# Two feed-forward layers on one Trainium2 core: the last pair of the opening block computed plainly, and half of the second weight matrix's rows loaded through POOL's queue

## The chip, the cores and the metric

The program runs on one core of a Trainium2 chip. The metric is the device time of one execution in microseconds; lower is better. Before the change three executions took 2122.06 us in the median (2121.51 to 2124.43). The engines are called PE (the matmul engine), DVE (vector), ACT (scalar), POOL and SP; SP issues most of the DMAs, POOL issues some.

## The reference, cut to what matters

Two layers over 256 tokens of width 2048: layer 0 mixes tokens with an mLSTM, layer 1 with an RG-LRU. Each layer ends in the same kind of feed-forward network, which takes more than half of the time and is where the change lies:

```python
def swiglu(x, w_in, w_out):
    g, u = jnp.split(x @ w_in, 2, axis=-1)
    return (jax.nn.silu(g) * u) @ w_out
...
        h = h + mix
        h = h + swiglu(rms_norm(h, norm_ffn[layer]), ffn_w_in[layer], ffn_w_out[layer])
    return rms_norm(h, norm_final)
```

`w_in` is 2048 x 11264 (gate and up part side by side), `w_out` is 5632 x 2048, all in float32.

## The kernel before, in words

**Split operands.** Every float32 operand is cut into a rounded part and a remainder, `hi` and `lo`. A product is three matmuls (`product`, L828 to L830): hi times hi, hi times lo, lo times hi. So each weight tile costs ACT a rounding copy (L264, `hi`) and DVE a subtraction (L265, `lo = raw - hi`) before PE can use it.

**Blocks and pairs.** `ffn` walks over 11 blocks `j` of 512 hidden columns. `inner` computes one block: it walks over 8 pairs `p` of 128-row chunks of `w_in`, and for each pair `pairs` loads four 128x512 pieces by two DMAs on SP's queue (L299). Two ways of multiplying a pair exist. A *plain* pair takes 8 products (24 matmuls) and needs the four pieces split (`whi`, `wlo`, 128x2048). Any other pair takes 7 products (21 matmuls) by a Strassen-like scheme, which needs three of the pieces split (`whix`, `wlox`) and four sums of pieces formed by DVE (`sum`, L308, L311, L312) and split in two halves (`whit`, `wlot`: the first half holds T1 and T3, the second T2 and T4). The set `BOTH` names the pairs that are plain in block 0; pair 0 is always plain. A plain pair of `BOTH` needs two more activation tiles, which `NormPairs.pair` makes in the mixer before (`more`, L489 to L495).

**The end of a block.** After the last Strassen-like pair (7), the sums P1, Q6 and P7 are final and ACT and DVE combine them (L863 to L866); after the block follow the rest, two Silu (L873, L876) and two products (L878). `turn_v` (L887) transposes the result for the second matmul.

**The second matmul in pieces.** `outs` cuts block j's part of `w_out` into eight pieces: quarter q of the output columns, token block b. One piece is 12 matmuls, and `between` puts one behind some product of each pair, so that the pieces of one block run inside the next. Pieces are summed in `h`: `o` is filled with `h` (L946), 12 matmuls add to it, and a copy on ACT writes it back (L957). Two weight tiles serve the pieces of a quarter. Tile 0 is split as above. Tile 1 is split in another way: ACT writes the rounded negative of the rows (L925, `wl`), an accumulating DMA from POOL's queue adds the rows from memory to it (L926), so that `wl` becomes the remainder without DVE; a second ACT copy writes `wh` (L927). `rawo` has one buffer for each tile, `wl` of tile 1 has two in turn.

**Order.** A scheduler puts the instructions of each engine in a fixed order by priorities; `after(...)` adds a rule that an instruction comes behind another on its engine. Each engine and each queue then runs strictly in that order, so a wait holds up all that stands behind it. SP's queue holds the loads of `w_in` and `w_out`; POOL's queue holds the accumulating DMAs and a few small operations.

**Parameters.** Small vectors are loaded as rows, transposed on PE and kept in three 128x128 tiles `cols` (L178 to L211).

Of the kernel before, what the change touches and what calls it, by code (L numbers as in the profile page):

```python
# [8 lines left out]
F32 = mybir.dt.float32  # L9
# [19 lines left out]

SEVENS = (1, 2, 3, 4, 5, 6, 7)  # L30

BOTH = (1, 2, 3, 4)

SHIFT = 48
PRODUCTS = (
# [9 lines left out]
def kernel(  # L45
# [129 lines left out]

    rows = pool_of("y").tile([P, 4, T], F32, tag="yh3", name="rows")
    rows = [rows[:, i, 0:P] for i in range(3)]
    cols = [const.tile([P, P], F32, name=f"cols{i}") for i in range(3)]  # L178
    part, at, used, par_rows = 0, 0, [0, 0, 0], []
    for name, src, n in par_src:  # L180
        if part == 0 and at or at + n > P:
            part, at = part + 1, 0
        par_rows.append((rows[part][at:at + n, :], src))
        par[name] = cols[part][:, at:at + n]
        at += n
        used[part] = at
    bif = const.tile([H, 2], F32, name="bif")

    gain0 = cols[0][:, 64:68]
    nc.scalar.dma_start(gain0, norm_mix[0].rearrange("(k p) -> p k", p=P)[:, 0:4])  # L190
    load_x()
    nc.scalar.dma_start(*par_rows.pop(0))
# [11 lines left out]
        return order  # L204

    def par_cols(i):
        n = used[i]
        pt = misc(f"par{i}")
        nc.tensor.transpose(pt[:, 0:n], rows[i][0:n, :], ident[0:n, 0:n])
        with tc.high_priority(offset=AHEAD):  # L210
            nc.vector.tensor_copy(cols[i][:, 0:n], pt[:, 0:n])  # L211


    pending = []
# [235 lines left out]
    class NormPairs(Norm):  # L450
# [10 lines left out]
        def pair(self, p):  # L461
            plain = p not in SEVENS
            k0, k1 = 2 * p, 2 * p + 1
            order = ((k0, 0), (k0, 1), (k1, 0), (k1, 1)) if plain else ((k1, 1), (k0, 0), (k0, 1), (k1, 0))
            n = 6 if plain else 7
            pt = misc(f"tr_{self.name}{p}").rearrange("p (s t) -> p s t", t=P)
            for i, (k, b) in enumerate(order):
                nc.tensor.transpose(pt[:, i, :], h[:, b, k * P:(k + 1) * P], ident)
            place, tag = ("c", "c") if "c" in pools else ("rawo", "raw0")
            c = pool_of(place).tile([P, 10 if place == "c" else 8, P], F32, tag=tag, name=f"c_{self.name}{p}")  # L470
            for k, sl in ((k0, slice(0, 2)), (k1, slice(2, 4))) if plain else ((k0, slice(1, 3)), (k1, slice(0, 4, 3))):
                nc.scalar.activation(c[:, sl, :], pt[:, sl, :], AF.Copy, scale=self.gain[:, k:k + 1])
            if plain:
                nc.vector.tensor_tensor(c[:, 4:6, :], c[:, 0:4:2, :], c[:, 1:4:2, :], op=ALU.subtract)
                src = c[:, 0:6, :]
            else:

                nc.vector.tensor_tensor(c[:, 4, :], c[:, 0, :], c[:, 2, :], op=ALU.subtract)
                nc.vector.tensor_tensor(c[:, 5, :], c[:, 3, :], c[:, 0, :], op=ALU.subtract)
                nc.vector.tensor_tensor(c[:, 6, :], c[:, 3, :], c[:, 4, :], op=ALU.subtract)  # L480
                nc.vector.tensor_tensor(c[:, 7, :], c[:, 1, :], c[:, 6, :], op=ALU.subtract)
                src = c[:, 1:8, :]

            rest = SHIFT if p == NK // 2 - 1 else 0
            xt = pool_of("x").tile([P, 2 * n * P + rest], F32R, tag=f"p{p}", name=f"p{p}_{self.name}")
            xt = xt[:, 0:2 * n * P].rearrange("p (s n t) -> p s n t", s=2, n=n)
            split(xt[:, 0], xt[:, 1], src)
            self.x.append(xt)
            if p in BOTH:  # L489

                nc.scalar.copy(c[:, 8, :], c[:, 0, :])
                nc.vector.tensor_tensor(c[:, 9, :], c[:, 1, :], c[:, 2, :], op=ALU.subtract)
                more = pool_of("more").tile([P, 2, 2, P], F32R, tag=f"m{p}", name=f"m{p}_{self.name}")
                split(more[:, 0], more[:, 1], c[:, 8:10, :])
                self.more[p] = more  # L495

        def parts(self, q):
# [309 lines left out]
    def ffn(layer, n, nxt):  # L807
# [24 lines left out]
        def inner(j, between):  # L832
# [9 lines left out]

            ds = fp.tile([P, 4, NB], F32, tag="ds", name=f"ds{j}")
            d0, d1, s0, s1 = (ds[:, i, :] for i in range(4))
            for p, ops in pairs(w, j, layer == 1):
                if is_plain(j, p):

# [4 lines left out]
                else:  # L852
                    seven = n.seven(p)
                    work = [
                        (c, seven[a], ops[b], p == SEVENS[-1])
                        for c, a, b in (LAST if p == SEVENS[-1] else PRODUCTS)
                    ]
                for i, job in enumerate(work):
                    add(*job)
                    between(j, p, i + 1 - len(work))  # L860
                if p == SEVENS[-1]:
                    with tc.high_priority(offset=AHEAD):
                        nc.scalar.copy(s0, ps["P1"])  # L863
                        nc.vector.tensor_tensor(d0, ps["Q6"], s0, op=ALU.subtract)
# [25 lines left out]
            with tc.high_priority(offset=AHEAD):  # L890
                split_store(hi[:, 2 * i:2 * i + 2, :], lo[:, 2 * i:2 * i + 2, :], pt)

        fresh = [True]

        def outs(j, hi, lo):

# [6 lines left out]
            def load(q, last):  # L903
# [9 lines left out]
                for i in range(2):  # L913
# [4 lines left out]
                        for what, dt, at in (("raw", F32, ""), ("whi", F32R, ""), ("wlo", F32R, spare))  # L918
                    )
                    src = wv[:, 2 * i:2 * i + 2, q * NB:(q + 1) * NB]  # L920
                    nc.sync.dma_start(raw, src)
                    with tc.high_priority(offset=AHEAD):
                        if i:

                            nc.scalar.activation(wl, raw, AF.Copy, scale=-1.0)  # L925
                            nc.gpsimd.dma_start(wl, src, accum_op=ALU.add)  # L926
                            nc.scalar.copy(wh, raw)  # L927
                        else:
# [3 lines left out]
            def piece(q, b, last=False):  # L932
# [20 lines left out]
                with tc.high_priority(offset=AHEAD):  # L953
                    if first:
                        nc.vector.tensor_tensor(hs, o, hs, op=ALU.add)
                    else:
                        nc.scalar.copy(hs, o)  # L957

            return [(piece, q, b) for q in range(4) for b in range(NT)]

# [266 lines left out]
```

## Time and profile before

| what | before |
|---|---|
| median of three executions | 2122.06 us |
| profiled execution, its own time | 2119.97 us |
| span of the profile | 2118.2 us |
| granted PE clock, mean | 0.998 |
| PE busy, share of the span | 2074.1 us, 98% |
| DVE busy | 1756.5 us, 83% |
| ACT busy | 1438.4 us, 68% |
| POOL busy | 135.4 us, 6% |
| DMA moved | 446.66 MB, 211 GB/s |

In the profile a row reads: line, engine, operation, output<-inputs, shape, count. "[8.66 <-DMA rawo]" behind a row of the timeline is the time that the engine sat idle before it, and what ended the wait. Matmuls overlap each other, and their ends are modelled: a matmul of 512 columns is shown as 0.39 us, but the starts of undisturbed ones stand 0.2267 us apart. The first feed-forward network runs from 398.5 us on, the second from 1402.2 us on.

### The profile page before, as it was taken

Reading aid. Unit: us, or ns where it says so; the run is one execution under the profiler, and the core shown is the slowest. Engines: PE = TensorE matmul, PEld = TensorE weight load, DVE = VectorE, ACT = ScalarE, POOL = GpSimd, SP = SyncE. Lnnn points to the kernel's source line nnn. Section 1 sums busy time; section 2 is a strip of 40 time slices with the busy share of each in tenths; the row PEclk is TensorE's granted clock in tenths of the full one; section 3 lists DMA queues with packets and bytes.
Section 4 is the critical chain, followed back from the end, with each engine's and each line's share of the span. In section 5 each row is a group of like instructions: output and inputs, shape, how many; then the busy total and the mean of one; then the engine's idle time right before and its main releaser. Section 6 shows DMA issues by size and latency. Waiting matters only on the chain.

```text
span 2118.2 us, 27777 instructions
## 1 busy us (share of the span) xinstructions
PE 2074.1 (98%) x10418; PEld 1737.8 (82%) x10418; DVE 1756.5 (83%) x1936; ACT 1438.4 (68%) x1749; POOL 135.4 (6%) x140
## 2 busy tenths in 40 slices
PE   9999999989999999999999999998999999999998
PEld 8988888867888888887879999886788887888886
DVE  6655556599999999999986788669999999999996
ACT  5444446557777777777764778655777777777775
POOL 0011110000000000000000000000000000000001
PEclk9999999999999999999999999999999999999999
DMA  7556666656877878888765666764788887878874
GB/s 224 170 163 178 179 185 218 192 165 194 243 239 235 231 229 239 237 236 230 230 189 160 193 189 188 228 203 154 209 245 231 235 232 222 242 231 248 238 222 156
DMA packets 233119, 446.66 MB, mean 211 GB/s; under 512 B 16328, under 2 KB 17048, under 8 KB 232856
## 3 DMA queue, kind: packets, MB, share of 16 engines
q1 hardware_dynamic: 211048, 402.92, 58.3%
q0 software_dynamic: 21216, 40.90, 12.3%
q8 instruction: 81, 1.33, 0.3%
q10 hardware_dynamic: 720, 1.07, 0.1%
q14 instruction: 54, 0.44, 0.1%
HBM read 442.74 MB, written 2.10 MB: 210 GB/s over the span
## 4 chain that ended last, share of the span: by engine, by line
PE 80%; ACT 7%; DVE 6%; DMA 4%; issue 3%; POOL 0%; ACTq 0%; POOLq 0%; SPq 0%; DVEq 0%
PE out L828 6%; PE out L829 6%; PE out L830 6%; PE P L829 5%; PE P L830 5%; PE P L828 5%; PE Q L828 5%; PE Q L829 5%; PE Q L830 4%; DMA rawo<-in_ffn_w_out_dram 4%; PE po L324 3%; PE po L326 3%; PE po L325 3%; DVE wlox L265 2%; DVE wlot L265 1%
## 5 line engine op out<-in xcount | busy, mean ns | idle before, releaser
L240 DVE TENSOR_TENSOR wlo<-raw,whi 128x1024 fp32r<-128x1024 f32 (+1 forms) x226 | 273.5, 1213 | 171.5 <-ACT whi L239 169.0
L264 ACT CAST whit<-sum 128x1024 fp32r<-128x1024 f32 x292 | 305.5, 1049 | 108.0 <-DVE sum L308 87.7
L265 DVE TENSOR_TENSOR wlot<-sum,whit 128x1024 fp32r<-128x1024 f32 x292 | 355.0, 1221 | 23.6 <-ACT whit L264 22.7
L239 ACT CAST whi<-raw 128x1024 fp32r<-128x1024 f32 (+1 forms) x226 | 234.4, 1042 | 196.0 <-PE po L326 43.2
L828 PE MATMUL out<-whio,hh 128*128 128x512 f32 x704 | 275.1, 391 | 0.1
L829 PE MATMUL out<-wloo,hh 128*128 128x512 f32 x704 | 274.4, 390 | 0.0
L830 PE MATMUL out<-whio,hh 128*128 128x512 f32 x704 | 274.3, 390 | 0.0
L265 DVE TENSOR_TENSOR wlox<-raw,whix 128x1536 fp32r<-128x1536 f32 x146 | 256.0, 1754 | 13.8 <-ACT whix L264 13.2
L264 ACT CAST whix<-raw 128x1536 fp32r<-128x1536 f32 x146 | 216.0, 1480 | 26.0 <-PE P L830 22.3
L308 DVE TENSOR_TENSOR sum<-raw 128x1024 f32<-128x1024 f32 x146 | 178.6, 1224 | 10.0 <-DMA raw<-in_ffn_w_in_dram 5.9
L925 ACT ACTIVATE wloo<-rawo 128x1024 fp32r<-128x1024 f32 x78 | 82.8, 1062 | 144.3 <-DMA rawo<-in_ffn_w_out_dram 144.3
L926 POOL DMA_DIRECT2D wloo<-in_ffn_w_out_dram x78 | 94.0, 1206 | 1229.3 <-ACT wloo L925 918.9
L828 PEld LDWEIGHTS out<-whio,hh 128*128 128x128 f32 x704 | 132.1, 188 | 29.7 <-ACT out L946 1.2
L829 PEld LDWEIGHTS out<-wloo,hh 128*128 128x128 f32 x704 | 132.2, 188 | 28.0 <-DVE wloo L265 0.7
L830 PEld LDWEIGHTS out<-whio,hh 128*128 128x128 f32 x704 | 132.2, 188 | 27.7
L828 PE MATMUL Q<-whit,p_f 128*128 128x512 f32 x292 | 117.1, 401 | 12.5 <-ACT whit L264 12.5
L828 PE MATMUL P<-whix,p_f 128*128 128x512 f32 x292 | 114.8, 399 | 9.0 <-ACT whix L264 9.0
L264 ACT CAST whio<-rawo 128x1024 fp32r<-128x1024 f32 (+1 forms) x88 | 101.0, 1147 | 33.1 <-PE out L830 23.9
L265 DVE TENSOR_TENSOR wloo<-rawo,whio 128x1024 fp32r<-128x1024 f32 (+1 forms) x88 | 117.9, 1339 | 5.6 <-ACT whio L264 5.5
L829 PE MATMUL P<-wlox,p_f 128*128 128x512 f32 x292 | 115.3, 395 | 4.1 <-DVE wlox L265 3.8
L829 PE MATMUL P<-wlot,p_f 128*128 128x512 f32 x292 | 114.0, 390 | 1.7 <-DVE wlot L265 1.7
L830 PE MATMUL P<-whix,p_f 128*128 128x512 f32 x292 | 114.6, 393 | 0.0
(296 smaller groups left out, 5131.4 us busy)
## 6 DMA issues: line engine op xcount, KB each, us to landing
raw<-in_ffn_w_in_dram SPq DMA_DIRECT2D x352, 512.0 KB, 6.5
rawo<-in_ffn_w_out_dram SPq DMA_DIRECT2D x176, 512.0 KB, 5.7
raw<-in_m_w_in_dram SPq DMA_DIRECT2D x94, 512.0 KB, 3.8
wloo<-in_ffn_w_out_dram POOLq DMA_DIRECT2D x78, 512.0 KB, 6.3
raw<-in_r_w_in_dram SPq DMA_DIRECT2D x64, 512.0 KB, 4.3
raw<-in_m_w_out_dram SPq DMA_DIRECT2D x32, 512.0 KB, 3.7
raw<-in_r_w_out_dram SPq DMA_DIRECT2D x32, 512.0 KB, 4.5
gr<-in_r_gate_w_dram SPq DMA_DIRECT2D x8, 512.0 KB, 3.8
```

Of the source, the lines that this page charges most:

```text
L239: nc.scalar.copy(hi[:, i:i + step, 0:ncols], r)
L240: nc.vector.tensor_tensor(lo[:, i:i + step, 0:ncols], r, hi[:, i:i + step, 0:ncols].bitcast(F32), op=ALU.subtract)
L264: nc.scalar.copy(hi, src)
L265: nc.vector.tensor_tensor(lo, src, hi.bitcast(F32), op=ALU.subtract)
L308: nc.vector.tensor_tensor(t[:, 0:2, :], raw[:, 1:3, :], raw[:, 3:4, :].broadcast_to([P, 2, NB]), op=ALU.add)
L324: nc.tensor.matmul(o, lhsT=ah[:, bs], rhs=hi, start=(k == 0), stop=False)
L325: nc.tensor.matmul(o, lhsT=ah[:, bs], rhs=lo, start=False, stop=False)
L828: nc.tensor.matmul(o, lhsT=a[0], rhs=b[0], start=start, stop=False, **kw)
L829: nc.tensor.matmul(o, lhsT=a[0], rhs=b[1], start=False, stop=False, **kw)
L830: nc.tensor.matmul(o, lhsT=a[1], rhs=b[0], start=False, stop=stop, **kw)
L925: nc.scalar.activation(wl, raw, AF.Copy, scale=-1.0)
L926: nc.gpsimd.dma_start(wl, src, accum_op=ALU.add)
```

## The change

Six edits that hang together:

1. `BOTH` gets pair 7. In block 0 of each layer pair 7 is plain: 24 matmuls where 21 stood, no sums, one split of 128x2048. The last Strassen-like pair of that block is then 6 (`last`), and P1, Q6 and P7 are combined one pair earlier. The stop flags and the order of products follow.
2. The extra activation tiles are made in place in `c` (columns 0 and 1), so one ACT copy per pair of `BOTH` goes; pair 7 gets such a tile (`m7`).
3. The parameters lie in two `cols` tiles where three stood; with the smaller `c` this makes room for `m7`. As many transposes and copies as before.
4. The rows for tile 1 of the pieces are loaded by POOL's queue, not SP's.
5. The rounded negative of tile 1 (L925 before, L928 after) is put behind the copy back to `h` (L957, now L960) of the last piece but one that was written.
6. Line numbers move by one to three.

```diff
-BOTH = (1, 2, 3, 4)
+BOTH = (1, 2, 3, 4, 7)
...
-    cols = [const.tile([P, P], F32, name=f"cols{i}") for i in range(3)]
...
+    cols = [const.tile([P, P], F32, name=f"cols{i}") for i in range(2)]
...
-            c = pool_of(place).tile([P, 10 if place == "c" else 8, P], F32, tag=tag, name=f"c_{self.name}{p}")
+            c = pool_of(place).tile([P, 8, P], F32, tag=tag, name=f"c_{self.name}{p}")
...
-                nc.scalar.copy(c[:, 8, :], c[:, 0, :])
-                nc.vector.tensor_tensor(c[:, 9, :], c[:, 1, :], c[:, 2, :], op=ALU.subtract)
+                nc.vector.tensor_tensor(c[:, 1, :], c[:, 1, :], c[:, 2, :], op=ALU.subtract)
...
-                split(more[:, 0], more[:, 1], c[:, 8:10, :])
+                split(more[:, 0], more[:, 1], c[:, 0:2, :])
...
+            last = max(p for p in SEVENS if not is_plain(j, p))
...
-                        (c, seven[a], ops[b], p == SEVENS[-1])
-                        for c, a, b in (LAST if p == SEVENS[-1] else PRODUCTS)
+                        (c, seven[a], ops[b], p == (last if c in ("P7", "P1", "Q6") else NP - 1))
+                        for c, a, b in (LAST if p == NP - 1 else PRODUCTS)
...
-                if p == SEVENS[-1]:
+                if p == last:
...
-        fresh = [True]
+        fresh, copies = [True], []
...
-                    nc.sync.dma_start(raw, src)
+                    (nc.gpsimd if i else nc.sync).dma_start(raw, src)
...
-                            nc.scalar.activation(wl, raw, AF.Copy, scale=-1.0)
+                            with after(*copies[-2:-1]):
+                                nc.scalar.activation(wl, raw, AF.Copy, scale=-1.0)
                             nc.gpsimd.dma_start(wl, src, accum_op=ALU.add)
                             nc.scalar.copy(wh, raw)
...
-                        nc.scalar.copy(hs, o)
+                        copies.append(nc.scalar.copy(hs, o))
```

In the orders below a name such as `rawo011` reads: block 0, quarter 1, tile 1; `whix0_5` is block 0, pair 5; `whit4_7` block 4, pair 7; the number at the end is a buffer's.

POOL, at the start of the first feed-forward network, before:

```order
L440 TENSOR_TENSOR rstd_f0_3780<-ms_f0_3777,mhalf_93 128x2
L926 DMA wloo001_4215<-in_ffn_w_out_dram 128x2x512
L926 DMA wloo011_4333<-in_ffn_w_out_dram 128x2x512
L926 DMA wloo021_4461<-in_ffn_w_out_dram 128x2x512
L926 DMA wloo031_4598<-in_ffn_w_out_dram 128x2x512
```

and after:

```order
L923 DMA rawo001_4205<-in_ffn_w_out_dram 128x2x512
L442 TENSOR_TENSOR rstd_f0_3779<-ms_f0_3776,mhalf_93 128x2
L929 DMA wloo001_4207<-in_ffn_w_out_dram 128x2x512
L923 DMA rawo011_4323<-in_ffn_w_out_dram 128x2x512
L929 DMA wloo011_4325<-in_ffn_w_out_dram 128x2x512
L923 DMA rawo021_4451<-in_ffn_w_out_dram 128x2x512
```

The rows of the next quarter now stand behind the accumulating DMA of this one; SP's queue has lost these loads.

ACT, in block 0 of the first feed-forward network, from the second rounded negative on, before:

```order
L925 ACTIVATE wloo011_4333<-rawo011_4331 128x1024
L264 CAST p6_f0_3724<-c_f06_3717 128x896
L264 CAST whix0_5_3882<-raw0_5_3875 128x1536
L472 ACTIVATE c_f07_3763<-tr_f07_3758,cols1_97 128x256
L472 ACTIVATE c_f07_3763<-tr_f07_3758,cols1_97 128x2x128
L264 CAST p7_f0_3770<-c_f07_3763 128x896
L264 CAST whit0_5_3886<-sum0_5_3878 128x1024 x2
L264 CAST whio000_4208<-rawo000_4207 128x1024
L264 CAST whix0_6_3923<-raw0_6_3916 128x1536
L264 CAST whit0_6_3927<-sum0_6_3919 128x1024 x2
L264 CAST whix0_7_3961<-raw0_7_3954 128x1536
L264 CAST whit0_7_3965<-sum0_7_3957 128x1024
```

and after:

```order
L928 ACTIVATE wloo011_4325<-rawo011_4323 128x1024
L266 CAST whix0_5_3881<-raw0_5_3874 128x1536
L266 CAST p6_f0_3719<-c_f06_3712 128x896
L474 ACTIVATE c_f07_3758<-tr_f07_3753,cols0_96 128x256
L474 ACTIVATE c_f07_3758<-tr_f07_3753,cols0_96 128x2x128
L266 CAST whit0_5_3885<-sum0_5_3877 128x1024 x2
L266 CAST p7_f0_3765<-c_f07_3758 128x896
L266 CAST whix0_6_3922<-raw0_6_3915 128x1536
L266 CAST m7_f0_3769<-c_f07_3758 128x256
L266 CAST whit0_6_3926<-sum0_6_3918 128x1024 x2
L266 CAST whi0_7_3959<-raw0_7_3956 128x2048
```

The second negative still stands ahead of pair 5; the copy `whio000` has left the place ahead of pair 6, and pair 7 is one split.

ACT, in a later block (block 4, end of pair 6 and pair 7), before:

```order
L264 CAST whit4_6_5813<-sum4_6_5805 128x1024
L925 ACTIVATE wloo321_5970<-rawo321_5968 128x1024
L264 CAST whit4_7_5879<-sum4_7_5871 128x1024
L957 COPY h_73<-out310_5847 128x512
L264 CAST whit4_7_5879<-sum4_7_5871 128x1024
L946 COPY out311_5897<-h_73 128x512
L863 COPY ds4_5430<-P1_4_5525 128x512
```

and after:

```order
L266 CAST whit4_6_5805<-sum4_6_5797 128x1024
L266 CAST whix4_7_5867<-raw4_7_5860 128x1536
L266 CAST whit4_7_5871<-sum4_7_5863 128x1024
L960 COPY h_73<-out310_5839 128x512
L928 ACTIVATE wloo321_5962<-rawo321_5960 128x1024
L266 CAST whit4_7_5871<-sum4_7_5863 128x1024
L949 COPY out311_5889<-h_73 128x512
```

The negative `wloo321` has moved behind the copy of piece 310; it now stands between the two halves of pair 7.

ACT again, at the first Silu pair of the next block, before:

```order
L264 CAST whit5_1_6022<-sum5_1_6014 128x1024
L925 ACTIVATE wloo331_6107<-rawo331_6105 128x1024
L876 ACTIVATE ds4_5430<-ds4_5430,rstd_f0_3780 128x512
L957 COPY h_73<-out320_5975 128x512
L946 COPY out321_6041<-h_73 128x512
L264 CAST whit5_1_6022<-sum5_1_6014 128x1024
```

and after:

```order
L266 CAST whit5_1_6014<-sum5_1_6006 128x1024
L878 ACTIVATE ds4_5422<-ds4_5422,rstd_f0_3779 128x512
L266 CAST whit5_1_6014<-sum5_1_6006 128x1024
L960 COPY h_73<-out320_5967 128x512
L928 ACTIVATE wloo331_6099<-rawo331_6097 128x1024
```

The negative `wloo331` has left the place ahead of the second Silu and stands behind the copy of piece 320.

DVE, in block 4, pair 7, before:

```order
L265 TENSOR_TENSOR wlox4_7_5876<-raw4_7_5868,whix4_7_5875 128x1536
L265 TENSOR_TENSOR wlot4_6_5814<-sum4_6_5805,whit4_6_5813 128x1024
L308 TENSOR_TENSOR sum4_7_5871<-raw4_7_5868 128x1024
L311 TENSOR_TENSOR sum4_7_5871<-sum4_7_5871,raw4_7_5868 128x512
L312 TENSOR_TENSOR sum4_7_5871<-sum4_7_5871,raw4_7_5868 128x512
L265 TENSOR_TENSOR wlot4_7_5880<-sum4_7_5871,whit4_7_5879 128x1024 x2
```

and after:

```order
L267 TENSOR_TENSOR wlot4_6_5806<-sum4_6_5797,whit4_6_5805 128x1024
L310 TENSOR_TENSOR sum4_7_5863<-raw4_7_5860 128x1024
L267 TENSOR_TENSOR wlox4_7_5868<-raw4_7_5860,whix4_7_5867 128x1536
L313 TENSOR_TENSOR sum4_7_5863<-sum4_7_5863,raw4_7_5860 128x512
L267 TENSOR_TENSOR wlot4_7_5872<-sum4_7_5863,whit4_7_5871 128x1024
L314 TENSOR_TENSOR sum4_7_5863<-sum4_7_5863,raw4_7_5860 128x512
L267 TENSOR_TENSOR wlot4_7_5872<-sum4_7_5863,whit4_7_5871 128x1024
```

The third sum now stands behind the first half's subtraction, and nothing stands between it and the second half's.

PE, in block 4, at the start of pair 7, before:

```order
L830 MATMUL P1_4_5525<-whix4_7_5875,p7_f0_3770 128x512
L828 MATMUL P7_4_5553<-whit4_7_5879,p7_f0_3770 128x512
L828 MATMUL Q6_4_5557<-whit4_7_5879,p7_f0_3770 128x512
L829 MATMUL P7_4_5553<-wlot4_7_5880,p7_f0_3770 128x512
L830 MATMUL P7_4_5553<-whit4_7_5879,p7_f0_3770 128x512
L828 MATMUL Q5_4_5438<-whit4_7_5879,p7_f0_3770 128x512
```

and after:

```order
L831 MATMUL P1_4_5517<-whix4_7_5867,p7_f0_3765 128x512
L829 MATMUL P7_4_5545<-whit4_7_5871,p7_f0_3765 128x512
L830 MATMUL P7_4_5545<-wlot4_7_5872,p7_f0_3765 128x512
L831 MATMUL P7_4_5545<-whit4_7_5871,p7_f0_3765 128x512
L829 MATMUL Q6_4_5549<-whit4_7_5871,p7_f0_3765 128x512
L829 MATMUL Q5_4_5430<-whit4_7_5871,p7_f0_3765 128x512
```

The product of T2 (Q6), the first that needs the second half, now stands behind three matmuls of P7, not one.

More of the change, by code (lines that the diff above doesn't have):

```diff
@@ L177 @@
     rows = [rows[:, i, 0:P] for i in range(3)]
-    cols = [const.tile([P, P], F32, name=f"cols{i}") for i in range(3)]
[L179 to L186, printed above, removed]
+    cols = [const.tile([P, P], F32, name=f"cols{i}") for i in range(2)]
+    parts = [(0, 0, par_src[:1]), (0, 32, par_src[1:5]), (1, 0, par_src[5:])]
+    used, par_rows = [], []
+    for part, (c, c0, srcs) in enumerate(parts):
+        at = 0
+        for name, src, n in srcs:
+            par_rows.append((rows[part][at:at + n, :], src))
+            par[name] = cols[c][:, c0 + at:c0 + at + n]
+            at += n
+        used.append((cols[c][:, c0:c0 + at], at))
     bif = const.tile([H, 2], F32, name="bif")
-    gain0 = cols[0][:, 64:68]
+    gain0 = cols[0][:, 112:116]
     nc.scalar.dma_start(gain0, norm_mix[0].rearrange("(k p) -> p k", p=P)[:, 0:4])
@@ L206, in par_cols @@
     def par_cols(i):
-        n = used[i]
+        dst, n = used[i]
         pt = misc(f"par{i}")
@@ L210, in par_cols @@
         with tc.high_priority(offset=AHEAD):
-            nc.vector.tensor_copy(cols[i][:, 0:n], pt[:, 0:n])
+            nc.vector.tensor_copy(dst, pt[:, 0:n])
     pending = []
```

## The prediction

> **What bounds the kernel now.** I read first the busy time by stretches, cut at block 0, block 1 and blocks 2 to 10 of the first feed-forward network (the second repeats it; the fourth row is its block 0, where PE idles 7.15 us).
>
> ```profile
> core 0: us, PE busy (x) PEld busy (x) DVE busy (x) ACT busy (x) POOL busy (x), PEclk, DMA share, GB/s
> 398.50:458.20 59.70, 52.82 (x221) 41.58 (x222) 47.42 (x51) 32.71 (x34) 3.31 (x3) 0.97 0.66 203
> 458.20:517.80 59.60, 56.63 (x239) 42.67 (x238) 56.06 (x55) 38.88 (x42) 2.39 (x2) 1.00 0.57 173
> 517.80:1079.60 561.80, 554.86 (x2460) 453.59 (x2459) 528.20 (x510) 434.47 (x491) 42.09 (x35) 1.00 0.80 232
> 1402.20:1461.20 59.00, 51.85 (x218) 40.70 (x218) 46.95 (x51) 32.11 (x34) 3.13 (x3) 0.97 0.66 204
> ```
>
> PE idles 6.88 + 2.97 us in blocks 0 and 1, and 6.94 us in the nine later ones (0.77 each). DVE is at 94% in the last two stretches, ACT at 65 and 77%. So PE bounds the later blocks with DVE close behind it, and in block 1 DVE is the one that is full. In block 0 the clock is down too: 0.03 x 59.7 = 1.8 us.
>
> Next, what those waits are for, in blocks 2 to 10 (PE, then DVE, then ACT):
>
> ```profile
> PE Q L828 <- ACT whit L264: 5.6, 8, 0.9
> PE tv L887 <- DVE ds L878: 1.3, 3, 0.8
> DVE ds L878 <- ACT ds L876: 13.6, 8, 2.4
> DVE wlot L265 <- ACT whit L264: 9.7, 9, 1.1
> ACT wloo L925 <- DMA rawo<-in_ffn_w_out_dram: 58.6, 35, 3.5
> ```
>
> Once a block PE waits for the second half of pair 7, and in some blocks for the last product before `turn_v`. Behind both stands DVE, which waits for ACT; and ACT waits longest for rows that are not there yet, 58.6 / 35 = 1.7 us at each rounded negative. All that stands behind that negative is late by as much, among it the second Silu and the second halves. The same place at the end of a block, from the timelines of ACT and PE:
>
> ```profile
> 1688.81 1.06 ACT L925 ACTIVATE wloo<-rawo 128x1024 fp32r<-128x1024 f32 x1 [1.52 <-DMA rawo<-in_ffn_w_out_dram]
> 1690.62 1.05 ACT L264 CAST whit<-sum 128x1024 fp32r<-128x1024 f32 x1 [0.75 <-DVE sum L308]
> 1691.58 0.58 ACT L957 COPY h<-out 128x512 f32<-128x512 f32 x1
> 1692.05 1.04 ACT L264 CAST whit<-sum 128x1024 fp32r<-128x1024 f32 x1
> 1677.22 0.39 PE L828 MATMUL P<-whix,p_f 128*128 128x512 f32 x1
> 1689.91 0.39 PE L830 MATMUL out<-whio,hh 128*128 128x512 f32 x1
> 1691.95 0.39 PE L830 MATMUL P<-whix,p_f 128*128 128x512 f32 x1
> 1693.15 0.50 PE L828 MATMUL Q<-whit,p_f 128*128 128x512 f32 x1 [0.58 <-ACT whit L264]
> ```
>
> From 1677.22 to 1691.95 lie 65 starts: 0.2267 us a matmul. Q6 was due at 1692.40 (two behind 1691.95) and started at 1693.15: 0.75 us lost.
>
> For block 0 I read ACT's and DVE's timelines and the issues:
>
> ```profile
> 407.41 1.05 ACT L925 ACTIVATE wloo<-rawo 128x1024 fp32r<-128x1024 f32 x1
> 418.78 1.06 ACT L925 ACTIVATE wloo<-rawo 128x1024 fp32r<-128x1024 f32 x1 [8.66 <-DMA rawo<-in_ffn_w_out_dram]
> 420.58 1.48 ACT L264 CAST whix<-raw 128x1536 fp32r<-128x1536 f32 x1
> 431.37 1.05 ACT L264 CAST whio<-rawo 128x1024 fp32r<-128x1024 f32 x1 [3.66 <-DMA rawo<-in_ffn_w_out_dram]
> 432.32 1.47 ACT L264 CAST whix<-raw 128x1536 fp32r<-128x1536 f32 x1
> 433.82 1.76 DVE L265 TENSOR_TENSOR wlox<-raw,whix 128x1536 fp32r<-128x1536 f32 x1
> 435.50 2.35 DVE L265 TENSOR_TENSOR wlot<-sum,whit 128x1024 fp32r<-128x1024 f32 x2
> 437.89 1.23 DVE L308 TENSOR_TENSOR sum<-raw 128x1024 f32<-128x1024 f32 x1
> 440.70 0.69 DVE L311 TENSOR_TENSOR sum<-sum,raw 128x512 f32<-128x512 f32 x1
> 444.11 2.29 DVE L265 TENSOR_TENSOR wlo<-raw,whi 128x2048 fp32r<-128x2048 f32 x1 [0.99 <-ACT whi L264]
> 446.32 1.22 DVE L265 TENSOR_TENSOR wlot<-sum,whit 128x1024 fp32r<-128x1024 f32 x1
> 458.05 1.22 DVE L265 TENSOR_TENSOR wlot<-sum,whit 128x1024 fp32r<-128x1024 f32 x1
> 408.78 1.39 POOL L926 DMA_DIRECT2D wloo<-in_ffn_w_out_dram  x1 [5.49 <-ACT wloo L925]
> 409.42 0.42 SPq L921 DMA_DIRECT2D rawo<-in_ffn_w_out_dram  x1
> ```
>
> ACT stands still twice for rows that a later piece needs: 8.66 us ahead of pair 5, 3.66 us ahead of pair 6. PE pays here:
>
> ```profile
> PE P L828 <- ACT whix L264: 4.3, 3, 2.1
> PE P L829 <- DVE wlox L265: 1.7, 2, 1.3
> PE P L828 <- DVE ds L872: 1.6, 1, 1.6
> ```
>
> **The change part by part.**
>
> *Pair 7 plain in block 0 (twice).* PE gets 3 matmuls more: 3 x 0.2267 = 0.7 us. DVE loses the sums (1.23 + 0.69 + 0.69; L312 is as long as L311) and the splits (1.76 + 2 x 1.22), together 6.8, and gets 2.29 and some 0.6 for `m7` (two small operations; bounded by zero and twice the 0.69 of the 512-column sum): about 3.9 us less. ACT gets about as much less as its 1.47 + 2 x 1.05 stand above one longer copy. DVE is what PE waits for here, so this is on the path.
>
> *The order in block 0.* `whio000` leaves the place ahead of pair 6, and the 3.66 us wait with it. It turns up behind the splits of block 1's first pairs, where its rows have long landed. The 8.66 us wait stays, since the second negative still stands ahead of pair 5. Its rows now come through POOL's queue, behind the first accumulating DMA. No transfer of plain rows through that queue is in the trace, so I bound it by both kinds:
>
> ```profile
> DMA to landing us min/median/max: 3.6/5.7/9.5
> DMA to landing us min/median/max: 5.9/6.3/11.1
> ```
>
> (rows through SP; accumulating DMAs through POOL). At best the rows land as before, at 418.7. At worst they follow the accumulation, which itself needs the 11.1 us from 408.78, and then 3.6 more: 423.5. I take 421, some 2 us later, since the accumulation and the rows share a queue, but SP's has two loads fewer.
>
> From 421, ACT: negative, `whix` of pair 5 to 423.4. DVE: `wlox` 5 to 425.1, pair 6's activations and pair 7's small differences 2.0, `wlot` 5 2.3, pair 7's activations 1.0, three sums and one difference 2.7, `wlox` 6 1.7: 434.8, where it ended at 435.6 before. Then `wlot` 6 2.3, `m7` 0.4, pair 7 2.3, one evacuation 0.6, block 1's pair 0 2.2: 442.6. Before, the last operand of that set ended at 446.32 + 1.22 = 447.5. Behind it stand the end of the block and block 1's pair 1: eight operations of 0.69, two of 1.23, then 1.76 and 2.35, to about 454.5; before, that last `wlot` ended at 458.05 + 1.22 = 459.3. So DVE is 5 us ahead, at the row where it is full for the next 60 us, and PE follows it: 5 us for each network, its three matmuls being inside PE's idle time. Rows at 418.7 make it 7, rows at 423.5 2.5. PE still waits some 2.5 us at pair 6.
>
> A page of the Trainium skill bears on that wait: "TensorE: Matmul & The Clock Gate", section "Part 1: The HAM clock gate", says that PE falls to half its clock after an idle window of about 3.4 us. By it a single wait of 2.5 us would keep the clock, and 1.8 us of PE time would come back; by the row above (0.97 in a stretch whose longest wait was 2.1 us) it may not. DVE sets the time there, so the sum is the same by both.
>
> *Negative behind the copy, blocks 2 to 10.* The second Silu goes ahead of the negative, so DVE's 13.6 us and PE's 1.3 us for it go. At pair 7 the negative now stands between the halves: a cost. The copy needs piece 310's last matmul: 1689.91 + 0.39 = 1690.30. Then copy, negative and second half, 0.58 + 1.06 + 1.04: the half is there at 1692.98 if nothing else holds ACT. Q6 stands behind three P7 matmuls now, due at 1691.95 + 4 x 0.2267 = 1692.86. So 0.1 us is left of 0.75. But DVE forms the third sum later (behind the first half's 1.22), and then waits for ACT with nothing between; about one more wait of 1.1 us a block beside the nine it has, against 13.6 / 9 = 1.5 us won. DVE has that little to spare, so I credit 0.55 of the 0.77 us: 9 x 0.55 = 5 us for each network. The ends: all of the 6.94 us and the refill behind each wait, 9 us; and nothing, -1, if DVE falls back.
>
> *Rows through POOL's queue, blocks 2 to 10.* What an issue costs POOL shows the group of the accumulating DMAs:
>
> ```profile
> L926 POOL DMA_DIRECT2D wloo<-in_ffn_w_out_dram x78 | 94.0, 1206 | 1229.3 <-ACT wloo L925 918.9
> ```
>
> 78 loads at the same 1.2 us are 94 us more on POOL, which idles; SP loses 78 issues of the 0.42 us above, which nothing waits for. Behind each load on POOL stands only the next accumulation. The negative starts as soon as the rows land, and the copy behind it ended 3.3 us later (1688.81 to 1692.16); rows may be that much later before ACT waits again. The accumulation starts about 3 us later, and its piece is two pieces on.
>
> *In-place tiles, parameters.* One ACT copy less for each of four pairs, one pair more; same transposes. ACT is not waited for there: nothing.
>
> Sum: 2 x (5 + 5) = 20 us. The profiled execution took 2119.97 us, 2.1 below the median of 2122.06; from the median, 2102.
>
> **The rivals.**
>
> *Slower: rows late at pair 7.* If POOL's queue brings the rows over 3.3 us later than SP's, the negative waits between the halves of pair 7, and each us beyond is a us of PE, 18 times. It decides from 20 / 18 = 1.1 us on, that is rows 4.4 us later than now. An accumulation's 11.1 in place of 5.7 would be 5.4 later: 2.1 x 18 = 38 us lost, 2122 - 20 + 38 = 2140. Against it: half of the accumulations land within 6.3. Chance 0.07.
>
> *No change.* The wait in front of the negative is only moved, DVE stays the bound of the later blocks at 94% and loses 1 us there, and the rows of block 0 land at 423.5, which leaves 2.5: 2 x 1.5 = 3 us, 2119. Chance 0.11. A rule of the Trainium skill speaks for it: "DMA: Bandwidth & Descriptors", section "Issuing engines are not separate DMA queues", says that issuing from several engines saves no more than the sequencer's time to issue. By it the new queue is worth 78 times the 0.42 us of SP's issue, off the path. The row of ACT's 58.6 us says that order, not bandwidth, is what is short.
>
> *One half only.* Block 0 or the later blocks gain, not both: 2112. Chance 0.17.
>
> *All of it.* Every PE wait of the later blocks goes, and block 0 keeps its early rows: 2 x (7 + 9) = 32, 2090. Chance 0.15.
>
> **How the numbers follow.** The forecast, 2102, has 0.50. A measurement of this kernel can tell about 0.2%, 4 us, from no change. Faster by more: 0.50 + 0.15 + 0.17 = 0.82; within: 0.11; slower: 0.07. The range leaves out the slower case, most of no change and the far end of the best: 2087 to 2117.
>
> **What would show it.** Right: the wait of ACT for rows is gone in later blocks but for a us or two, and stays at 8 to 12 us once in each block 0; DVE no longer waits for the second Silu; PE's wait for `whit` shrinks to about 0.2 us a block; block 1's first `turn_v` comes some 6 us earlier. Wrong: an ACT wait of over a us in front of the negative at pair 7, a PE wait for the second half as long as before, or rows landing in block 0 after 423.

## The result, and the profile after

The changed kernel took 2094.86 us in the median (2094.32 to 2095.76), beside 2121.78 us for the kernel before on the same chip: a ratio of 0.9871, with a 95% interval from 0.9854 to 0.9888. It is about 27 us faster, where 20 were forecast. The profiled execution has a span of 2093.1 us, 25.1 less than before.

Busy time by stretches of the changed kernel: block 0, block 1 and blocks 2 to 10 of the first network, then the same of the second. A block's stretch begins at the first `turn_v` for its predecessor, as before.

```profile
core 0: us, PE busy (x) PEld busy (x) DVE busy (x) ACT busy (x) POOL busy (x), PEclk, DMA share, GB/s
397.50:450.40 52.90, 50.71 (x219) 41.34 (x220) 40.65 (x45) 33.45 (x34) 4.87 (x5) 0.97 0.72 223
450.40:510.60 60.20, 57.51 (x242) 43.28 (x241) 58.27 (x58) 38.98 (x42) 3.91 (x4) 1.00 0.64 195
510.60:1068.20 557.60, 554.08 (x2463) 454.34 (x2462) 526.89 (x510) 431.86 (x491) 68.29 (x70) 1.00 0.81 234
1390.40:1440.90 50.50, 48.92 (x220) 39.97 (x219) 40.45 (x46) 33.30 (x34) 4.72 (x5) 1.00 0.75 235
1440.90:1501.50 60.60, 57.78 (x243) 43.20 (x242) 58.65 (x58) 39.17 (x43) 3.91 (x4) 1.00 0.63 194
1501.50:2056.70 555.20, 553.87 (x2463) 454.20 (x2462) 527.04 (x510) 431.21 (x492) 68.29 (x70) 1.00 0.81 236
```

The stretch of block 0 went from 59.7 to 52.9 us; PE idles 2.2 us in it where it idled 6.9. Part of this is where the cut falls: in the records 108 matmuls of block 0's stretch write P where 114 did, and 98 of block 1's where 92 did. So six matmuls, 1.4 us, have moved from ahead of the first `turn_v` to behind it. Block 1 is 0.6 us longer for that, although PE idles 2.7 us in it where it idled 3.0; only the sum of the two blocks compares like with like. Blocks 2 to 10 took 561.8 us and take 557.6, and PE idles 3.5 us where it idled 6.9. The same cut of both kernels through the whole span:

| stretch | before | after | gain |
|---|---|---|---|
| up to the first network | 398.5 | 397.5 | 1.0 |
| first network, blocks 0 and 1 | 119.3 | 113.1 | 6.2 |
| first network, blocks 2 to 10 | 561.8 | 557.6 | 4.2 |
| second mixer | 321.7 | 322.2 | -0.5 |
| second network, blocks 0 and 1 | 119.7 | 111.1 | 8.6 |
| second network, blocks 2 to 10 | 561.5 | 555.2 | 6.3 |
| rest | 35.7 | 36.4 | -0.7 |

The first product of the second network before starts at 1401.3 us, not at the 1402.2 given as its begin above; the table goes by 1401.3.

What the waits are for in blocks 2 to 10 of the first network (PE, DVE, ACT):

```profile
PE Q L829 <- ACT whit L266: 3.0, 5, 1.5
DVE wlot L267 <- ACT whit L266: 17.8, 16, 2.7
ACT wloo L928 <- DMA rawo<-in_ffn_w_out_dram: 4.6, 6, 1.5
```

ACT's wait for rows, 58.6 us before, is 4.6. DVE's 13.6 us for the second Silu no longer appear, nor does PE's wait ahead of `turn_v`. DVE waits longer for `whit`, 17.8 in place of 9.7. At pair 7 the order on ACT is now copy, negative, second half:

```profile
1669.82 0.59 ACT L960 COPY h<-out 128x512 f32<-128x512 f32 x1 [1.42 <-PE out L831]
1670.30 1.06 ACT L928 ACTIVATE wloo<-rawo 128x1024 fp32r<-128x1024 f32 x1
1671.30 1.05 ACT L266 CAST whit<-sum 128x1024 fp32r<-128x1024 f32 x1
1672.40 0.73 PE L829 MATMUL Q<-whit,p_f 128*128 128x512 f32 x2
```

The negative starts without a wait, the half is there at 1672.35, and Q6 follows at 1672.40 with no idle time ahead of it.

In block 0, ACT, DVE and POOL's queue:

```profile
418.38 1.06 ACT L928 ACTIVATE wloo<-rawo 128x1024 fp32r<-128x1024 f32 x1 [8.73 <-DMA rawo<-in_ffn_w_out_dram]
431.39 1.75 DVE L267 TENSOR_TENSOR wlox<-raw,whix 128x1536 fp32r<-128x1536 f32 x1
408.31 1.24 POOL L929 DMA_DIRECT2D wloo<-in_ffn_w_out_dram  x1 [5.44 <-ACT wloo L928]
409.23 1.09 POOL L923 DMA_DIRECT2D rawo<-in_ffn_w_out_dram  x1
433.20 0.50 PE L830 MATMUL P<-wlox,p_f 128*128 128x512 f32 x1 [2.19 <-DVE wlox L267]
```

The 8.7 us wait ahead of pair 5 stays, `wlox` of pair 6 ends at 433.1, and PE waits once, 2.19 us. The cost of POOL's issues over the whole program:

```profile
L929 POOL DMA_DIRECT2D wloo<-in_ffn_w_out_dram x78 | 94.0, 1205 | 702.9 <-ACT wloo L928 678.2
L923 POOL DMA_DIRECT2D rawo<-in_ffn_w_out_dram x78 | 59.1, 758 | 755.3 <-ACT whio L930 362.6
```

### The profile page after: what moved, and what is told of

Read it like the earlier page. It is cut to its first block, busy times and chain, and to the rows that moved or that the text cites. A ratio compares the mean times of both kernels' runs of the same rounds, so it can differ in the third digit from the quotient of the medians.

```text
span 2093.1 us, 27909 instructions
## 1 busy us (share of the span) xinstructions
PE 2068.5 (99%) x10424; PEld 1738.0 (83%) x10424; DVE 1746.0 (83%) x1930; ACT 1429.0 (68%) x1739; POOL 195.9 (9%) x218
## 4 chain that ended last, share of the span: by engine, by line
PE 73%; DVE 11%; issue 6%; ACT 4%; DMA 4%; POOL 1%; SPq 0%; ACTq 0%; POOLq 0%; DVEq 0%
PE out L829 5%; PE out L830 5%; PE out L831 5%; PE P L830 5%; PE P L831 5%; PE P L829 5%; PE Q L829 4%; PE Q L830 4%; PE Q L831 4%; DMA rawo<-in_ffn_w_out_dram 3%; DVE wlot L267 2%; DVE wlox L267 2%; PE po L328 2%; PE po L327 2%; PE po L326 2%
## 5 line engine op out<-in xcount | busy, mean ns | idle before, releaser
L266 ACT CAST whit<-sum 128x1024 fp32r<-128x1024 f32 x288 | 301.3, 1050 | 182.4 <-DVE sum L310 144.2
L267 DVE TENSOR_TENSOR wlot<-sum,whit 128x1024 fp32r<-128x1024 f32 x288 | 348.9, 1221 | 36.0 <-ACT whit L266 34.6
L960 ACT COPY h<-out 128x512 f32<-128x512 f32 x154 | 89.8, 583 | 65.3 <-PE out L831 65.2
L923 POOL DMA_DIRECT2D rawo<-in_ffn_w_out_dram x78 | 59.1, 758 | 755.3 <-ACT whio L930 362.6
L829 PE MATMUL P<-whix,p_f 128*128 128x512 f32 x288 | 112.3, 398 | 2.7 <-ACT whix L266 2.7
L830 PE MATMUL Q<-wlot,p_f 128*128 128x512 f32 x288 | 113.2, 397 | 0.1
```

Of the source, the lines that this page charges most:

```text
L266: nc.scalar.copy(hi, src)
L267: nc.vector.tensor_tensor(lo, src, hi.bitcast(F32), op=ALU.subtract)
L829: nc.tensor.matmul(o, lhsT=a[0], rhs=b[0], start=start, stop=False, **kw)
L830: nc.tensor.matmul(o, lhsT=a[0], rhs=b[1], start=False, stop=False, **kw)
L923: (nc.gpsimd if i else nc.sync).dma_start(raw, src)
L960: copies.append(nc.scalar.copy(hs, o))
```

## The experiments

The question was which of the parts brings the 27 us. The change has three: pair 7 in block 0 (with tiles and parameters), the queue, and the place of the negative. The first four kernels take them apart. The edits on pair 7, tiles and parameters are those of the diff above and are not repeated.

**Pair 7 alone.** Of the diff, without these:

```diff
-                    (nc.gpsimd if i else nc.sync).dma_start(raw, src)
+                    nc.sync.dma_start(raw, src)
...
-                            with after(*copies[-2:-1]):
-                                nc.scalar.activation(wl, raw, AF.Copy, scale=-1.0)
+                            nc.scalar.activation(wl, raw, AF.Copy, scale=-1.0)
```

> The kernel before with the edits to pair 7, the tiles and the parameters alone; rows on SP's queue, negative where the planner puts it. Theory A (the parts add up; block 0 and what block 1 gets from it are worth 6 us in the first network and 8 in the second, and 1 us comes at the front): 2121.8 - 15 = 2107 us, block 1's first turn_v 6 to 8 us earlier, blocks 2 to 10 as before at about 62.4 us each. Theory B (a good part of the opening's gain belongs to the rows on POOL's queue, since SP has fewer loads ahead of pair 6's and 7's rows): 2112 to 2116 us.

Measured: 2102.34 us, ratio 0.9918 (0.9904 to 0.9931), 5 us below theory A. The stretches of the first network:

```profile
398.00:446.70 48.70, 48.70 (x219) 40.23 (x220) 40.62 (x45) 33.44 (x34) 3.31 (x3) 1.00 0.75 241
446.70:507.60 60.90, 58.28 (x244) 43.57 (x243) 58.63 (x58) 39.20 (x42) 2.39 (x2) 1.00 0.60 191
507.60:1069.80 562.20, 554.85 (x2462) 453.78 (x2460) 528.25 (x511) 434.32 (x491) 42.10 (x35) 1.00 0.80 232
```

Block 0 takes 48.7 us, 4.2 less than in the changed kernel, and PE does not idle in it at all. Blocks 2 to 10 are as before (562.2). So pair 7 is worth 10 us a network by itself, and something else in the change takes part of it back. Theory B had the sign of the queue's part wrong.

**Rows on POOL's queue and the negative behind the copy, without pair 7.**

```diff
-BOTH = (1, 2, 3, 4, 7)
+BOTH = (1, 2, 3, 4)
```

> The changed kernel without pair 7 in the opening block (rows on POOL's queue and the negative behind the copy are kept). Theory A (the parts add up): blocks 2 to 10 at 62.0 us each as in the changed kernel, 4 + 6.5 us less, 2121.8 - 10.5 = 2111 us; block 0 as before with its two waits of ACT. Theory B (the later blocks gain only because DVE leaves the opening with a lead): 2116 to 2122 us.

Measured: 2106.83 us, ratio 0.9935 (0.9923 to 0.9948). Theory A, and 4 us below it: the later blocks gain without a lead from the opening (mostly 61.9 us a block).

**The queue alone**, in the kernel before:

```diff
-                    nc.sync.dma_start(raw, src)
+                    (nc.gpsimd if i else nc.sync).dma_start(raw, src)
```

> The kernel before with one line changed: rows of the accumulating half through POOL's queue. In blocks 2 to 10 ACT's order stays that of before, the negative ahead of the second Silu. Theory A (what matters is the order on ACT, not the queue): ACT goes on waiting for rows, 50 us or more a network, DVE for the second Silu; 2119 to 2123 us. Theory B (the wait of SP's queue for whio, 353.9 us in 72 waits, holds the loads behind it back, and freeing it is the gain): 2110 to 2115 us, ACT's wait for rows falls by more than half.

Measured: 2219.7 us, ratio 1.0474 (1.0458 to 1.0490): 99 us slower, which neither theory had. ACT's wait over the whole program was 144.3 us before; here it is

```profile
ACT wloo L925 <- DMA rawo<-in_ffn_w_out_dram: 251.4, 78, 6.4
```

and the stretch of blocks 2 to 10 of the first network reads

```profile
529.10:1129.60 600.50, 574.06 (x2455) 457.88 (x2454) 527.73 (x506) 431.73 (x491) 68.20 (x70) 0.98 0.74 215
```

At a negative of the queue-alone kernel (ACT, POOL, SP) it looks like this:

```profile
668.15 1.05 ACT L927 CAST whio<-rawo 128x1024 fp32r<-128x1024 f32 x1
669.50 0.75 POOL L921 DMA_DIRECT2D rawo<-in_ffn_w_out_dram  x1 [9.77 <-ACT whio L927]
669.75 0.37 SPq L299 DMA_DIRECT2D raw<-in_ffn_w_in_dram  x1
675.37 1.06 ACT L925 ACTIVATE wloo<-rawo 128x1024 fp32r<-128x1024 f32 x1 [3.32 <-DMA rawo<-in_ffn_w_out_dram]
```

and in the kernel before (ACT, SP):

```profile
680.04 1.05 ACT L927 CAST whio<-rawo 128x1024 fp32r<-128x1024 f32 x1
681.12 0.37 SPq L921 DMA_DIRECT2D rawo<-in_ffn_w_out_dram  x1
681.61 0.39 SPq L299 DMA_DIRECT2D raw<-in_ffn_w_in_dram  x1
685.62 1.07 ACT L925 ACTIVATE wloo<-rawo 128x1024 fp32r<-128x1024 f32 x1 [1.67 <-DMA rawo<-in_ffn_w_out_dram]
```

On SP the load starts right behind `whio` and ahead of the next load of `w_in`. On POOL it starts 0.3 us later, its issue takes 0.75 us instead of 0.37, and by its end SP has issued a load of `w_in`. Over the 76 negatives that have a predecessor in their network, worked out from the timelines, the median from the end of `whio` to the start of the negative is 4.53 us with SP and 6.16 us with POOL. Another weight load's issue comes between the end of `whio` and the end of the rows' issue 60 times with POOL and never with SP. At these 60 the negative is 1.7 us later with POOL (median of the differences from the same negative with SP); at the other 16 it is 0.4 us earlier, although POOL's longer issue is in them too. These 1.6 us stand on ACT ahead of what DVE and PE wait for, four times a block: blocks 2 to 10 took 600.5 us, 4.3 more for each; block 1 lost 12 us. Not all of it is late rows as such. In those nine blocks PE idles 26.4 us in place of 6.9, and by the granted clock, 0.98, up to 0.02 x 600.5 = 12 of the 38.7 us are PE running slower behind its waits.

**The negative alone**, in the kernel before, rows on SP's queue:

```diff
-                            nc.scalar.activation(wl, raw, AF.Copy, scale=-1.0)
+                            with after(*copies[-2:-1]):
+                                nc.scalar.activation(wl, raw, AF.Copy, scale=-1.0)
```

(and `copies` kept as in the diff).

> The kernel before with the negative put behind the copy alone; rows stay on SP's queue. Theory A (order is all): 2121.8 - 10.5 = 2111 us, as with both. Theory B (the later negative lets whio end later, SP's queue stands longer in front of the next rows and the rows of w_in behind them come late): 2115 to 2125 us, with PE or ACT waits for raw that are not in the trace of before.

Measured: 2105.39 us, ratio 0.9935 (0.9922 to 0.9947), theory A and more. It gives as much as with the queue over the whole program, and more in blocks 2 to 10: 7.1 and 7.4 us in the two networks, beside 4.5 and 3.0 in the kernel with rows on POOL's queue, which has the new tiles too. Blocks 2 to 10 of the first, and ACT's wait over the whole program:

```profile
517.00:1071.70 554.70, 553.79 (x2461) 453.80 (x2460) 526.27 (x510) 431.33 (x491) 42.10 (x35) 1.00 0.81 235
```

```profile
ACT wloo L926 <- DMA rawo<-in_ffn_w_out_dram: 19.7, 4, 9.1
```

PE idles 0.9 us in nine blocks, and ACT waits for rows four times in the whole program, and not once in blocks 2 to 10 of the first network. The order is all of this gain. The median from `whio` to the negative is 7.79 us here, so rows that need 4.5 or 6.2 us would mostly be there in both cases.

So the queue was the suspect for what the changed kernel lost against the sum of its parts. The second group tested that, and whether the 8.7 us wait in block 0 is worth removing.

**The changed kernel with its rows on SP's queue.**

```diff
-                    (nc.gpsimd if i else nc.sync).dma_start(raw, src)
+                    nc.sync.dma_start(raw, src)
```

> The changed kernel with all its rows back on SP's queue: pair 7 plain and the negative behind the copy are kept. Theory A (the two parts add up and the queue only costs: in block 0 it puts the rows behind the first accumulating DMA, which makes PE wait 2 us): 0.992 x 0.9935 = 0.985 of the kernel before, about 2091 us, no PE wait of over 1 us in block 0, first turn_v of block 1 near 447 us. Theory B (the parts overlap, and the queue costs nothing once the negative is behind the copy): 2095 us as the changed kernel.

Measured: 2087.22 us, ratio 0.9842 (0.9827 to 0.9857). Theory A, even 4 us below it. Block 0, block 1 and blocks 2 to 10:

```profile
398.20:446.90 48.70, 48.70 (x218) 40.27 (x219) 40.62 (x45) 33.47 (x34) 3.32 (x3) 1.00 0.75 240
446.90:507.70 60.80, 58.24 (x245) 43.71 (x244) 58.76 (x59) 39.02 (x42) 2.39 (x2) 1.00 0.61 191
507.70:1062.40 554.70, 553.68 (x2462) 453.82 (x2460) 526.24 (x510) 431.28 (x491) 42.09 (x35) 1.00 0.80 235
```

In block 0, SP's queue and the negative that waited 8.73 us:

```profile
409.61 0.37 SPq L923 DMA_DIRECT2D rawo<-in_ffn_w_out_dram  x1
410.08 10.95 SPq L301 DMA_DIRECT2D raw<-in_ffn_w_in_dram  x6
414.86 1.06 ACT L928 ACTIVATE wloo<-rawo 128x1024 fp32r<-128x1024 f32 x1 [4.55 <-DMA rawo<-in_ffn_w_out_dram]
```

On SP the rows are issued behind two loads of `w_in` and ahead of six; in the kernel before four stood ahead. Counted from the network's first product (398.20 here, 397.50 in the changed kernel), the negative starts at 16.7 us in place of 20.9, 4.2 us sooner than through POOL, where the rows are issued behind an accumulating DMA while SP's loads run. Which of these two delays them was not tried apart. The queue is the one edit between the two kernels, so it is the difference between no idle time of PE in block 0 and 2.2 us of it.

**The changed kernel with block 0's two negatives held back** behind the copy of P1 in that block:

```diff
-                            with after(*copies[-2:-1]):
+                            with after(*(copies[-2:-1] or starts)):
...
+                        if j == 0:
+                            starts.append(s0_copy)
```

(`s0_copy` is the ACT copy of P1, L865.)

> The changed kernel with block 0's two negatives held back behind the copy of P1 in that block, so that ACT no longer stands 8.7 us for rows ahead of pair 5, and one accumulating DMA and one load move from 408-419 us to about 435-445 us. Theory A (that wait is what keeps DVE back in block 0, and DVE's lead pays in blocks 0 and 1): wlox of pair 6 ends some 6 us earlier, PE's 2.3 us wait and the half clock behind it go; 4 to 6 us per network, about 2085 us. Theory B (the moved DMAs meet block 1's own loads, or block 1's waits have other causes): 2091 to 2097 us.

Measured: 2101.55 us, ratio 0.9908 (0.9893 to 0.9923). Block 0 did become shorter (48.7 us, PE never idle), but block 1 took 65.6, and the kernel is slower than the changed one: nearer to B, and beyond it. ACT, DVE and what PE waits for in block 1:

```profile
446.98 1.06 ACT L930 ACTIVATE wloo<-rawo 128x1024 fp32r<-128x1024 f32 x1 [5.14 <-DMA rawo<-in_ffn_w_out_dram]
449.62 0.75 DVE L882 SCALAR_TENSOR_TENSOR ds<-ds,rstd_f 128x512 f32<-128x512 f32 x1 [5.16 <-ACT ds L880]
PE tv L891 <- DVE ds L882: 3.3, 1, 3.3
```

The second negative now waits 5.14 us in block 1 ahead of the second Silu; DVE waits for that Silu, and PE for DVE.

**Both: rows on SP's queue, and the two negatives held back** (the two edits above together).

> Both: rows on SP's queue and block 0's negatives held back. Theory A (with rows on SP PE waits for nothing in block 0 any more; what is left is DVE's lead into block 1, whose matmuls lose about 6 us): 3 to 5 us per network below the kernel with rows on SP alone, about 2083 us. Theory B (block 1's waits are set by ACT's order there and not by DVE's lead): no change against rows on SP alone, about 2091 us.

Measured: 2093.47 us, ratio 0.9869 (0.9851 to 0.9886), 6 us slower than rows on SP alone. Both theories missed it. ACT's timeline:

```profile
414.91 1.48 ACT L266 CAST whix<-raw 128x1536 fp32r<-128x1536 f32 x1 [6.03 <-PE P L831]
446.93 1.06 ACT L930 ACTIVATE wloo<-rawo 128x1024 fp32r<-128x1024 f32 x1 [3.88 <-DMA rawo<-in_ffn_w_out_dram]
447.90 1.03 ACT L266 CAST whit<-sum 128x1024 fp32r<-128x1024 f32 x1
```

Without the negative in front, `whix` of pair 5 still waits until 414.91, for PE to free its buffer. With the negative in front it started at 415.84, but there the network's first product stood at 398.20, here at 397.27: counted from it, `whix` starts at 17.64 us in both, and block 0 takes 48.7 us in both. The wait of 4.55 us for rows had been covered entirely. And the second negative now waits 3.88 us in block 1, ahead of a `whit`; the `hh` of `turn_v` behind them come late, and PE waits:

```profile
PE P L829 <- DVE hh L544: 1.8, 1, 1.8
```

Block 1 takes 64.3 us in place of 60.7; beside this wait, PE's clock is at 0.97 in it, which is up to 0.03 x 64.3 = 1.9 us. Moving a wait out of a covered place put it into an uncovered one.

**Rows in two loads of 256 KB on SP's queue.** This was meant as a dose: rows a little later, but still ahead of SP's next load.

```diff
-                    nc.sync.dma_start(raw, src)
+                    if i:
+                        for c in range(2):
+                            nc.sync.dma_start(raw[:, c, :], src[:, c, :])
+                    else:
+                        nc.sync.dma_start(raw, src)
```

In the kernel before:

> The kernel before with one edit: rows of the accumulating half come in two loads of 256 KB in place of one of 512 KB, both on SP's queue, so they are complete some 0.4 us later (one more issue) but still go ahead of SP's next load. ACT's order in blocks 2 to 10 is that of before. Theory A (with the negative ahead of the second Silu each us by which rows are late goes to PE; the queue alone made them 1.64 us later and a block 4.5 us longer): about 1.2 us a block, 2121 + 24 = 2145 us. Theory B (POOL's queue cost time because SP's other loads ran ahead of it and took bandwidth, not because rows were late): 2119 to 2124 us.

Measured: 2124.56 us, ratio 1.0014 (1.0005 to 1.0024). The dose was not given: the median from `whio` to the negative is 4.51 us, as with one load, and ACT's wait for rows is 146.5 us beside 144.3. Two halves with one more issue are complete as early as one load. So it tells neither theory's price of late rows. (The kernel is 2 us slower all the same; where these come from stays open.) It does say that 0.4 us more of issue alone need not make rows late. With the 60 and 16 negatives above, that leaves the loads of `w_in` that go ahead as the larger part of POOL's 1.6 us; this is read from the timelines and was not shown by a run of its own.

In the kernel with pair 7 and the negative behind the copy:

> The same two loads of 256 KB on SP's queue, in the kernel with pair 7 plain and the negative behind the copy. Theory A (behind the copy the negative has over 3 us to spare, so later rows cost nothing): as the kernel with one load on SP, 2087 us, within 4. Theory B (late rows cost PE wherever the negative stands): 2105 to 2112 us.

Measured: 2093.66 us, ratio 0.9862 (0.9849 to 0.9875), between the theories and 7 us above the kernel with one load on the same chip (2086.6, below). Blocks 2 to 10 are as in that kernel (555.2 us, from 511.3 to 1066.5). The loss is in block 0, 52.8 us in place of 48.7: the half load of the second negative fell behind four loads of `w_in` on SP, and that negative moved behind `whix`, where it starts at 423.06 after a wait of 5.19 us. PE then waits 2.2 us for `wlox` of pair 6, and its granted clock is 0.50 from 433.68 to 437.10. SP's issues:

```profile
409.76 3.31 SPq L301 DMA_DIRECT2D raw<-in_ffn_w_in_dram  x4
413.12 0.64 SPq L925 DMA_DIRECT2D rawo<-in_ffn_w_out_dram  x1
```

**The changed kernel and the one with rows on SP, side by side on one chip.**

> The changed kernel as it is, beside the next one on the same chip: 2095 us.

> The changed kernel with rows on SP's queue, again, beside the changed kernel. If POOL's queue costs the change something, 2087 us, 6 to 8 below the changed kernel; if the earlier difference came from the chip, the same as it.

Measured: 2095.63 us (0.9873, 0.9860 to 0.9887) and 2086.6 us (0.9831, 0.9818 to 0.9845). The queue costs the changed kernel 9.0 us. In the profiles of this pair the cost lies in the two blocks 0 (2.6 and 2.0 us) and in blocks 2 to 10 (3.3 and 1.9). The kernel with pair 7 and the negative behind the copy, and all its rows on SP's queue, beats both.

## Why the prediction was right, and where its terms were off

The direction and the two places were right, and the time lies inside the range. The sum, 20 us, came out at 27 because two of its terms were too small and one, which was put at nothing, is a loss. That the time lies well inside the range is in part luck: the two parts with rows on SP bring 34 and 36 us in two measurements (2087, the very edge of the range), and the loss that the sum did not have took 9 of them back.

**Pair 7 in block 0, forecast 5 us a network.** In the changed kernel blocks 0 and 1 gain 6.2 and 8.6 us. The steps held: `wlox` 6 ended at 433.1 (forecast 434.8); PE waited 2.2 us at pair 6 (forecast 2.5); the 3.66 us wait for `whio000` is gone and the long one stays. The three matmuls more are not inside PE's idle time, as the sum had it: behind 433.2 PE never idles in block 0, so they are 0.7 us of it. The second network gains 2.4 us more than the first; 1.7 of it is the clock, granted at 0.50 for 3.41 us in both networks before and now in the first alone. The step that failed is the best case for the rows, "at best the rows land as before, at 418.7". The new order on SP puts two loads of `w_in` ahead of them where four stood: with rows on SP the negative starts at 414.7 to 414.9, not 418.8, and pair 7 alone is worth 9.7 and 10.3 us (blocks 0 and 1 took 109.6 us in place of 119.3, and 109.4 in place of 119.7). In the changed kernel POOL's queue takes part of that back: the negative started at 418.38, which, counted from the network's first product, is 0.6 us later than before, where the sum took some 2.

**The negative behind the copy, forecast 5 us a network.** 4.2 and 6.3 us in the changed kernel, 7.1 and 7.4 us alone with rows on SP (561.8 to 554.7, 561.5 to 554.1). The mechanism is the one described: the Silu goes ahead, the half arrives 0.05 us before Q6. Mis-sized is what DVE would lose to its new waits: I let them take 1.9 of the 6.9 us. They are there, 17.8 us in place of 9.7, and as many with rows on SP (17.2), where PE idles 1.0 us in nine blocks. So they lie in DVE's spare time.

**Rows through POOL's queue, forecast nothing in the later blocks.** This step failed. An issue costs POOL 0.76 us, not the 1.2 us of an accumulation, but that is not what matters. The margin of 3.3 us at pair 7 was real, and with it rows 1.6 us later are nearly free; hence the changed kernel does not lose 99 us. But not every negative has that margin: ACT still waited 4.6 us in six places of blocks 2 to 10, PE idles 3.5 us there, against 1.0 with rows on SP, and block 0 has no copy to stand behind. Together 9.0 us. The rival *rows late at pair 7* had the right mechanism with a threshold of 4.4 us; in the order before, where ACT waits for rows at most negatives already, there is no such margin, and 1.6 us cost 99.

The rule that the prediction weighed, the Trainium skill, "DMA: Bandwidth & Descriptors", section "Issuing engines are not separate DMA queues", says that another engine's queue saves only the time to issue. That the queue brings nothing agrees: in three pairs of kernels that differ in it alone, the one with rows on POOL's queue is 99, 8 and 9 us slower. That it is therefore worth nothing either way does not follow. What leaving the queue gave up here is, by the timelines, the place of the rows ahead of SP's other loads.

**The clock.** The other rule, the Trainium skill, "TensorE: Matmul & The Clock Gate", section "Part 1: The HAM clock gate", has the clock fall after an idle window of about 3.4 us; as the prediction read it, a single shorter wait keeps the clock. In the changed kernel PE's wait of 2.19 us ended at 433.20, and the granted clock fell all the same. In the repeat of the same kernel a wait of 2.18 us at the same place did not bring it down (the changed kernel, then the repeat):

```profile
434.72:438.13 3.41, 3.41 (x10) 2.64 (x9) 3.23 (x3) 2.02 (x2) 0.00 (x0) 0.50 0.97 358
434.11 0.50 PE L830 MATMUL P<-wlox,p_f 128*128 128x512 f32 x1 [2.18 <-DVE wlox L267]
434.10:441.00 6.90, 6.89 (x30) 5.61 (x31) 6.90 (x6) 5.11 (x5) 0.00 (x0) 1.00 0.84 249
```

Block 0 took 52.9 us in the one and 51.3 in the other. A wait of 1.34 us in block 1 was followed by half a clock in the kernel with rows on SP and the negatives held back, and not in the one with rows on SP alone:

```profile
486.27 0.73 PE L829 MATMUL P<-whix,p_f 128*128 128x512 f32 x2 [1.34 <-ACT whix L266]
488.22:491.63 3.41, 3.41 (x9) 2.67 (x10) 3.34 (x4) 2.40 (x4) 1.20 (x1) 0.50 0.67 255
485.11 0.74 PE L829 MATMUL P<-whix,p_f 128*128 128x512 f32 x2 [1.34 <-ACT whix L266]
485.11:492.00 6.89, 6.78 (x27) 4.99 (x28) 6.62 (x6) 5.61 (x7) 1.20 (x1) 1.00 0.60 169
```

So the prediction was right to doubt the rule: waits well under 3.4 us can cost half the clock for 3.41 us. But the length of the wait alone does not decide it, and what else does stays open.

**The rivals.** *No change* and *one half only* fell, since each half is faster alone (0.9918 and 0.9935). *All of it*, 2090, needed all waits of the later blocks gone and the rows of block 0 early; that is close to what the kernel with rows on SP is, at 2087.

## What to carry to other kernels

A load that an in-order engine waits for should keep its place ahead of less urgent loads: through another queue it came behind them here, and 1.6 us a load cost 99 us where the waiting instruction stood ahead of critical work. Put the instruction that waits behind the work that does not depend on it first; then look whether the load still needs moving. And before a long wait is moved away, look at what would hold the next instruction in its place: a wait of 4.55 us was worth nothing, and cost 6 where it was put.

## What the runs showed of the hardware that was not expected

- A plain load of 512 KB costs POOL 0.758 us to issue, an accumulating one 1.205 us; the same plain load costs SP 0.37 us in the rows above, and starts 0.27 us sooner behind ACT's copy.
- The same load of rows, issued at 409.2 us on POOL behind an accumulation and at 409.6 us on SP ahead of six other loads, let the negative start at 418.38 and 414.86 us.
- One load of 512 KB and two of 256 KB on the same queue let the waiting instruction start equally early (4.53 and 4.51 us in the median from the copy that frees the tile).
- PE's granted clock was 0.50 for 3.41 us after a single wait of 2.19 us in one execution of a kernel and stayed at 1.00 after one of 2.18 us at the same place in another; after 1.34 us it fell in one kernel and not in another.
